# The causal mask of an attention block added by VectorE in PSUM, in place of a matmul of the identity with the mask

## The chip, the cores and the metric

The kernel runs on one core of a Trainium2 chip. The metric is the device time of one execution in microseconds (us), taken as the median of several runs. Engines: PE is TensorE's matmul stream and PEld its weight loads, DVE is VectorE, ACT is ScalarE, POOL is GpSimd, and SP is the queue from which every DMA of this kernel is issued. SBUF is the on-chip memory, PSUM the buffer that matmuls write.

## What is computed

Two layers of a decoder trunk with four token mixers in parallel. The part that matters here is branch B, causal attention with 8 heads over 1024 tokens, with 96 columns per query and key:

```
def one_block(args):
    q_blk, blk = args
    s = jnp.einsum('bhtd,bshd->bhts', q_blk, k).astype(jnp.float32) * scale
    query_pos = blk * ATTN_BLOCK + jnp.arange(ATTN_BLOCK)
    s = jnp.where(key_pos[None, :] <= query_pos[:, None], s, -jnp.inf)
    p = jax.nn.softmax(s, axis=-1).astype(v.dtype)
    return jnp.einsum('bhts,bshd->bthd', p, v)
```

Queries are taken in blocks of 128. Block t sees keys 0 to 128(t+1)-1, and only its last 128 columns, the diagonal block, need a mask.

## The kernel before

**Precision.** Operands are split into a high and a low part, and a product is three matmuls (high by high, high by low, low by high) accumulated in PSUM. Names ending in h and l are such parts: fh and fl are the two parts of the queries or keys of a head, bh and bl (wh and wl) those of a weight block.

**Attention.** `attention` runs over 8 heads and two halves b of the sequence, 16 steps to a layer. A step has a front and a back. The front, for the four query tiles t = 4b to 4b+3 of the next step, is `attn_scores` (three matmuls for each 512 columns into a tile named mm, then the mask, the row maximum mx on DVE at L1054, and ACT's nm, the maximum times the scale) and `attn_probs` (ACT's exponential into a tile pr, read straight from the PSUM tile mm). There are two mm buffers, so scores of tile t+2 wait until the exponential of tile t has been read out. The back, `attn_values`, transposes the four pr tiles on PE (L1087) into a PSUM tile tr, copies tr on ACT to the high part of pT, subtracts on DVE (L96) to get its low part, and multiplies both with the values v into the tile pv. There are two tr buffers. The 8 heads by 8 query tiles by 2 layers make 128 tiles.

**The mask.** A 128x128 bf16 tile `maskb` holds 0 on and below the diagonal and -1e30 above it. The last matmul of each score tile multiplies the bf16 identity with it and adds the result onto the diagonal block.

**Background.** While attention runs, the kernel also computes gate branches that later stages need (`background`). Each is two half blocks of 24 matmuls into a PSUM tile bg, a DVE product into bgx, ACT's tanh, and for the gate of branch B three more DVE operations. The last of these multiplies bgx with bgr, the inverse row sums of the softmax, which take a way through memory: a reciprocal and a copy (rows) on DVE, a DMA to riscr, and a DMA back that spreads them over the partitions (L164). br is the raw weight block of a background, with a single buffer, bh its cast on DVE and bl its low part, made by POOL.

**What sets the order.** The program is written in the order of the source. A scheduler with its own estimates of durations then sets the order of each engine's queue; background matmuls have a low priority and are put where it expects PE to wait. Each engine, and SP, works through its queue in that order, and an instruction that waits holds up everything behind it. A change of one instruction therefore moves others.

Of the kernel before, what the change touches and what calls it, by code (L numbers as in the profile page):

```python
# [15 lines left out]
MUL, ADD, SUB = ALU.mult, ALU.add, ALU.subtract  # L16

P = 128
# [26 lines left out]
class Trunk:  # L45
# [990 lines left out]
    def attn_scores(self, head, t, qt, kT):  # L1036

        nc = self.nc
        kh, kl = kT
        at = head % 2 * 8 + t  # L1040
        sc, nsc, sm = [x[:, at:at + 1] for x in (self.qs[head // 2], self.nqs[head // 2], self.asum[head // 2])]
        n = (t + 1) * P
        qh, ql = [x[0:96, t * P:(t + 1) * P] for x in qt]
        ps = self.mm()
        for c0 in range(0, n, 512):
            w = max(min(512, n - c0), 256)
            o = ps[:, c0:c0 + w]
            last = c0 + 512 >= n
            self.mmr(o, qh, kh[0:96, c0:c0 + w], True, False)
            self.mmr(o, qh, kl[0:96, c0:c0 + w], False, False)  # L1050
            self.mmr(o, ql, kh[0:96, c0:c0 + w], False, not last)
        self.mmr(ps[:, n - P:n], self.identb, self.maskb, False, True)
        mx, nm = self.ss(1, "mx"), self.ss(1, "nm")
        nc.vector.reduce_max(out=mx, in_=ps[:, 0:n], axis=AX.X)  # L1054
        self.act(nm, mx, AF.Identity, scale=nsc)
        return ps, n, nm, sc, sm
# [610 lines left out]
```

## Time and profile before

| | |
|---|---|
| median of 3 runs | 2439.56 us (2437.25 to 2441.05) |
| the profiled execution | 2440.25 us |
| its span, first to last instruction | 2438.5 us |
| mean granted TensorE clock | 0.988 |
| attention of layer 0 | about 516 to 755 us |
| attention of layer 1 | about 1700 to 1932 us |

The two stretches of attention are where the changed lines run. The busy time of PE counts a matmul until its modelled end, which reaches into the next one: two matmuls in a row start 0.23 us apart when they have 512 columns, though each is shown as 0.39 us long. What a matmul costs is therefore read from the distance between starts, and a wait that is shorter than the overlap doesn't show as idle time.

### The profile page before, as it was taken

The numbers are of one execution on the slowest core, as the hardware profiler recorded it, in microseconds if no ns is written. First come the engines' busy times: TensorE is split into PE (matmuls) and PEld (weight loads), VectorE is DVE, ScalarE is ACT, GpSimd is POOL, SyncE is SP. The second block draws the span as 40 slices with busy tenths as digits, with TensorE's granted clock in tenths as the row PEclk, the third lists the DMA queues.
The fourth block names the chain that finished last, engine by engine and source line by source line (L and its number), as shares of the span: only waits on it lengthen the run. The fifth ranks groups of instructions, "written<-read, shape, count | busy, mean of one in ns | idle before, by whom it ended". The sixth has DMA issues, their size and how long they took to land. (4 is left out here: it accounts for less than half of the span.)

```text
span 2438.5 us, 28178 instructions
## 1 busy us (share of the span) xinstructions
PE 2325.2 (95%) x11174; PEld 1855.2 (76%) x11174; DVE 1215.9 (50%) x1871; ACT 706.5 (29%) x1233; POOL 775.0 (32%) x605
## 2 busy tenths in 40 slices
PE   7998889989999999999999888999999999999999
PEld 5766677867778888888877666787777888888887
DVE  6455784366676323236244556714666652233351
ACT  4121253247762101101111213522577420111010
POOL 3533113432304214342435421143322132244411
PEclk9999999999999999999999999999999999999999
DMA  4226343242332112222432363413423211122342
GB/s 153 75 93 184 115 138 102 82 123 79 95 106 66 61 44 70 69 77 105 156 100 73 96 188 108 139 49 103 125 83 109 80 44 52 56 92 79 103 156 69
DMA packets 91700, 237.56 MB, mean 97 GB/s; under 512 B 25200, under 2 KB 34352, under 8 KB 91568
## 3 DMA queue, kind: packets, MB, share of 16 engines
q1 hardware_dynamic: 91568, 235.76, 30.4%
q8 instruction: 88, 1.44, 0.2%
q14 instruction: 44, 0.36, 0.1%
HBM read 175.27 MB, written 60.46 MB: 97 GB/s over the span
## 5 line engine op out<-in xcount | busy, mean ns | idle before, releaser
L96 POOL TENSOR_TENSOR wl<-wr,wh 128x1024 fp32r<-128x1024 f32 (+3 forms) x125 | 295.9, 2367 | 946.1 <-DVE wh L152 634.7
L176 PE MATMUL mm<-xh,wh 128*128 128x512 f32 x1216 | 378.7, 392 | 9.1 <-ACT xh L106 8.7
L152 DVE CAST wh<-wr 128x1024 fp32r<-128x1024 f32 (+2 forms) x110 | 78.4, 713 | 618.6 <-PE mm L176 539.8
L176 PE MATMUL mm<-xh,wl 128*128 128x512 f32 x1216 | 376.1, 390 | 0.8 <-POOL wl L96 0.8
L176 PE MATMUL mm<-xl,wh 128*128 128x512 f32 x1216 | 376.8, 390 | 0.0
L176 PEld LDWEIGHTS mm<-xh,wh 128*128 128x128 f32 x1216 | 227.3, 188 | 59.9 <-ACT xh L106 8.7
L176 PEld LDWEIGHTS mm<-xh,wl 128*128 128x128 f32 x1216 | 228.3, 188 | 49.7 <-POOL wl L96 1.6
L176 PEld LDWEIGHTS mm<-xl,wh 128*128 128x128 f32 x1216 | 228.4, 188 | 49.0 <-issue 0.8
L176 PE MATMUL bg<-xh,bh 128*128 128x512 f32 x576 | 229.2, 416 | 15.5 <-DVE bgx L96 15.5
L176 PE MATMUL bg<-xl,bh 128*128 128x512 f32 x576 | 226.3, 411 | 0.0
L176 PE MATMUL bg<-xh,bl 128*128 128x512 f32 x576 | 224.1, 409 | 1.0 <-POOL bl L96 1.0
L96 POOL TENSOR_TENSOR bl<-br,bh 128x1024 fp32r<-128x1024 f32 x36 | 96.4, 2678 | 317.0 <-DVE bh L152 203.3
L106 ACT ACTIVATE cmn<-cmn,bmh 128x1024 f32<-128x1024 f32 x44 | 50.6, 1151 | 440.7 <-DVE cmn L96 440.7
L96 DVE TENSOR_TENSOR pT<-tr,pT 128x512 fp32r<-128x512 f32 x224 | 125.6, 571 | 42.8 <-ACT pT L106 42.1
L176 PEld LDWEIGHTS bg<-xh,bh 128*128 128x128 f32 x576 | 111.8, 195 | 46.0 <-DVE bgx L96 25.6
L176 PE MATMUL pv<-pT,v 128*128 128x512 f32 (+3 forms) x384 | 134.0, 388 | 7.9 <-DVE pT L96 5.1
L106 ACT ACTIVATE pT<-tr 128x512 fp32r<-128x512 f32 x224 | 111.0, 505 | 86.6 <-PE tr L1087 77.3
L176 PEld LDWEIGHTS bg<-xh,bl 128*128 128x128 f32 x576 | 111.1, 193 | 24.9 <-issue 3.2
L1054 DVE TENSOR_REDUCE mx<-mm 128x1 f32<-128x128 f32 (+7 forms) x128 | 96.5, 754 | 64.5 <-PE mm L176 63.7
L176 PEld LDWEIGHTS bg<-xl,bh 128*128 128x128 f32 x576 | 111.3, 194 | 21.8 <-issue 4.0
L106 ACT ACTIVATE pr<-mm,nm,qs 128x128 f32<-128x128 f32 (+7 forms) x128 | 106.3, 830 | 0.9
L1087 PE MATMUL tr<-ident,pr 128*128 128x128 f32 x576 | 97.9, 275 | 0.3 <-ACT pr L106 0.2
(449 smaller groups left out, 4173.7 us busy)
## 6 DMA issues: line engine op xcount, KB each, us to landing
wr<-in_w_cm_dram SPq DMA_DIRECT2D x76, 512.0 KB, 3.6
br<-in_w_cm_dram SPq DMA_DIRECT2D x36, 512.0 KB, 3.7
bgscr<-bgx SPq DMA_DIRECT2D x20, 512.0 KB, 3.1
gate<-bgscr SPq DMA_DIRECT2D x20, 512.0 KB, 5.6
ysscr<-bgx SPq DMA_DIRECT2D x16, 512.0 KB, 2.6
br<-ysscr SPq DMA_DIRECT2D x16, 512.0 KB, 3.4
wr<-in_w_out_dram SPq DMA_DIRECT2D x16, 512.0 KB, 3.7
bgr<-riscr SPq DMA_DIRECT2D x24, 256.0 KB, 4.8
```

Source lines behind the costliest of these rows:

```text
L96: (eng or self.nc.vector).tensor_tensor(out=out, in0=x, in1=y, op=op)
L106: self.nc.scalar.activation(out, x, f, **k)
L152: self.nc.vector.tensor_copy(hi[:, :n], raw)
L176: self.nc.tensor.matmul(out, lhsT, rhs, start=start, stop=stop)
L1054: nc.vector.reduce_max(out=mx, in_=ps[:, 0:n], axis=AX.X)
L1087: nc.tensor.transpose(pt[:, k * P:(k + 1) * P], pts[k][:, st * P:(st + 1) * P], self.ident)
```

## The change

The mask matmul is gone, and the last score matmul closes the accumulation. DVE adds maskb (bf16, SBUF) onto the diagonal 128x128 of the PSUM tile, in place, and the row maximum follows as before. `tt` is the helper at L95 and L96 that issues a tensor_tensor on DVE, so the new operation is recorded at L96.

```
             w = max(min(512, n - c0), 256)
             o = ps[:, c0:c0 + w]
-            last = c0 + 512 >= n
             self.mmr(o, qh, kh[0:96, c0:c0 + w], True, False)
             self.mmr(o, qh, kl[0:96, c0:c0 + w], False, False)
-            self.mmr(o, ql, kh[0:96, c0:c0 + w], False, not last)
-        self.mmr(ps[:, n - P:n], self.identb, self.maskb, False, True)
+            self.mmr(o, ql, kh[0:96, c0:c0 + w], False, True)
+        self.tt(ps[:, n - P:n], ps[:, n - P:n], self.maskb, ADD)
```

The scheduler then orders the queues anew. Three places in layer 0 show it. Numbers in the names tell tiles apart and are the same in both programs; after the change, lines below the edit are one lower.

DVE, in the third head, where the scores of the tiles mm_4349 and mm_4371 are reduced. Before:

```order
L96 TENSOR_TENSOR pT_4335<-tr_4330,pT_4335 128x512
L96 TENSOR_TENSOR bgx_4535<-bg_4536,rsb_557 128x512
L96 TENSOR_TENSOR pT_4344<-tr_4340,pT_4344 128x384
L1054 TENSOR_REDUCE mx_4357<-mm_4349 128x1
L96 TENSOR_TENSOR pT_4366<-tr_4363,pT_4366 128x256
L1054 TENSOR_REDUCE mx_4379<-mm_4371 128x1
```

The same place after the change:

```order
L96 TENSOR_TENSOR pT_4335<-tr_4330,pT_4335 128x512
L1053 TENSOR_REDUCE mx_4325<-mm_4317 128x1
L96 TENSOR_TENSOR pT_4344<-tr_4340,pT_4344 128x384
L96 TENSOR_TENSOR mm_4349<-mm_4349,maskb_218 128x128
L1053 TENSOR_REDUCE mx_4357<-mm_4349 128x1
L96 TENSOR_TENSOR pT_4366<-tr_4363,pT_4366 128x256
L96 TENSOR_TENSOR pT_4385<-tr_4383,pT_4385 128x128
L96 TENSOR_TENSOR mm_4371<-mm_4371,maskb_218 128x128
```

In 90 of the 128 tiles the add stands directly ahead of its reduction; in the others something comes between, mostly one pT operation (as for mx_4325, which before stood ahead of pT_4335) or a product into bgx. The product into bgx_4535 has moved to another place.

PE, at the change from half 0 to half 1 of the same head's values, between the scores of mm_4399 and mm_4408, the first two tiles of the next step. Before:

```order
L1087 MATMUL tr_4426<-ident_204,pr_4390 128x128
L176 MATMUL bg_4562<-xl_23_135,bh_4531 128x512
L176 MATMUL bg_4562<-xh_22_134,bl_4532 128x512
L176 MATMUL bg_4562<-xh_25_144,bh_4531 128x512
L176 MATMUL bg_4562<-xl_26_145,bh_4531 128x512
L176 MATMUL bg_4562<-xh_25_144,bl_4532 128x512
L176 MATMUL mm_4408<-fh_4296,wh_4288 128x256
```

The same place after the change:

```order
L1086 MATMUL tr_4426<-ident_204,pr_4390 128x128
L176 MATMUL bg_4562<-xh_28_154,bh_4531 128x512
L176 MATMUL bg_4562<-xl_29_155,bh_4531 128x512
L176 MATMUL bg_4562<-xh_28_154,bl_4532 128x512
L176 MATMUL bg_4562<-xh_31_164,bh_4531 128x512
L176 MATMUL bg_4562<-xl_32_165,bh_4531 128x512
L176 MATMUL bg_4562<-xh_31_164,bl_4532 128x512
L176 MATMUL bg_4562<-xh_34_174,bh_4531 128x512
L176 MATMUL bg_4562<-xl_35_175,bh_4531 128x512
L176 MATMUL bg_4562<-xh_34_174,bl_4532 128x512
L176 MATMUL mm_4408<-fh_4296,wh_4288 128x256
```

Nine background matmuls stand ahead of mm_4408 where five stood; the others of the nine stood a little earlier, ahead of mm_4399.

SP, the DMA queue, after the row sums of a pair of heads are written to riscr. Before:

```order
L1074 DMA riscr<-rows_4526 16x128
L1019 DMA wr_4835<-q2scr 96x1024
L1239 DMA ybscr<-yb_4071 128x1024
L1019 DMA wr_4839<-kscr 96x1024
L1028 DMA wr_4845<-vscr 128x512
L1275 DMA bgy_4591<-ybscr 128x1024
L149 DMA br_6103<-in_w_cm_dram 128x1024
L164 DMA bgr_4594<-riscr 64x1024 x2
```

The same place after the change:

```order
L1073 DMA riscr<-rows_4526 16x128
L1019 DMA wr_4835<-q2scr 96x1024
L1238 DMA ybscr<-yb_4071 128x1024
L1019 DMA wr_4839<-kscr 96x1024
L1274 DMA bgy_4591<-ybscr 128x1024
L164 DMA bgr_4594<-riscr 64x1024 x2
L1028 DMA wr_4845<-vscr 128x512
```

The load of the row sums, bgr, has moved ahead of the load of a head's values (wr from vscr), and the load of a weight block (br) that stood ahead of it now comes before riscr.

## Rows read from the trace of the kernel before

**Rows 1.** The page's part 1: busy us (share of the span), instructions.

```profile
PE 2325.2 (95%) x11174; PEld 1855.2 (76%) x11174; DVE 1215.9 (50%) x1871; ACT 706.5 (29%) x1233; POOL 775.0 (32%) x605
```

**Rows 2.** Busy time by stretch: PE, PEld, DVE, ACT, POOL, then clock, DMA.

```profile
560.00:600.00 40.00, 39.17 (x220) 29.87 (x220) 27.03 (x44) 30.30 (x71) 13.47 (x7) 1.00 0.36 106
1690.00:1730.00 40.00, 34.00 (x149) 25.36 (x149) 26.84 (x52) 15.72 (x30) 13.08 (x6) 0.91 0.37 106
```

**Rows 3.** The tile view of maskb: count, durations (ns, min/median/max), first and last start.

```profile
L176 PE MATMUL mm<-maskb,identb x128: 229/232/330, 516.2 to 1907.9; 128*128 128x128 bf16 x128
```

**Rows 4.** Timeline of PE around two mask matmuls: start us, us, instruction.

```profile
562.41 0.23 PE L176 MATMUL mm<-maskb,identb 128*128 128x128 bf16 x1
562.48 0.39 PE L1087 MATMUL tr<-ident,pr 128*128 128x128 f32 x2
...
539.15 0.23 PE L176 MATMUL mm<-maskb,identb 128*128 128x128 bf16 x1
539.20 0.48 PE L176 MATMUL bg<-xh,bh 128*128 128x512 f32 x1
539.51 0.40 PE L176 MATMUL bg<-xl,bh 128*128 128x512 f32 x1
539.75 0.39 PE L176 MATMUL pv<-pT,v 128*128 128x512 f32 x1
```

**Rows 5.** Groups by shape on DVE, 580 to 680 us: busy us, mean ns.

```profile
L96 DVE TENSOR_TENSOR pT<-tr,pT 128x256 fp32r<-128x256 f32 x8 | 3.4, 419 | 0.3 <-ACT pT L106 0.3
L96 DVE TENSOR_TENSOR pT<-tr,pT 128x128 fp32r<-128x128 f32 x8 | 2.3, 285 | 2.0 <-ACT pT L106 2.0
```

**Rows 6.** Timeline: two dependent DVE operations, then one tile's chain.

```profile
527.02 0.23 DVE L103 SCALAR_TENSOR_TENSOR ry<-rt,ry 128x64 f32<-128x64 f32 x1
527.27 0.23 DVE L96 TENSOR_TENSOR ry<-ry,pre 128x64 f32<-128x64 f32 x1
...
562.68 1.09 DVE L1054 TENSOR_REDUCE mx<-mm 128x1 f32<-128x896 f32 x1 [0.53 <-PE mm L176]
```

**Rows 7.** Tile views of pr and pv: waits on them, us in total, times.

```profile
PEld mm L176: 18.3, 34
PE mm L176: 7.3, 6
...
DVE pT L96: 19.6, 45
```

**Rows 8.** Timeline: the bgr load of one gate, and who waits for it.

```profile
590.68 3.47 POOL L96 TENSOR_TENSOR bl<-br,bh 128x1024 fp32r<-128x1024 f32 x1
594.18 0.33 SPq L149 DMA_DIRECT2D br<-in_w_cm_dram  x1
594.62 1.09 SPq L164 DMA_DIRECT2D bgr<-riscr  x2
601.09 1.23 DVE L96 TENSOR_TENSOR bgx<-bgx,bgr 128x1024 f32<-128x1024 f32 x1 [2.98 <-DMA bgr<-riscr]
602.97 0.50 PE L176 MATMUL pv<-pT,v 128*128 128x512 f32 x1 [2.39 <-DVE pT L96]
```

**Rows 9.** Timeline: three more waits of PE that a gate of branch B causes.

```profile
651.21 0.50 PE L176 MATMUL pv<-pT,v 128*128 128x512 f32 x1 [1.52 <-DVE pT L96]
...
589.36 0.50 PE L176 MATMUL bg<-xh,bh 128*128 128x512 f32 x1 [0.54 <-DVE bgx L96]
...
638.43 0.50 PE L176 MATMUL bg<-xh,bh 128*128 128x512 f32 x1 [0.53 <-DVE bgx L96]
```

**Rows 10.** Timeline: waits of PE where each layer's attention begins.

```profile
528.79 0.44 PE L176 MATMUL mm<-fh,wh 96*128 96x384 f32 x1 [2.13 <-ACT pr L106]
...
537.58 0.50 PE L176 MATMUL mm<-fh,wh 96*128 96x512 f32 x1 [1.19 <-ACT pr L106]
...
1707.86 0.80 PE L176 MATMUL bg<-xh,bh 128*128 128x512 f32 x1 [2.99 <-DVE bgx L96]
...
1720.47 0.44 PE L176 MATMUL mm<-fh,wh 96*128 96x384 f32 x1 [2.65 <-ACT pr L106]
```

## Prediction, made before the changed kernel ran

> **What bounds the kernel now.** The page's busy times come first: PE is shown busy for 95% of the span, the next engine, DVE, for 50% [rows 1]. So an edit that takes work off PE and gives it to DVE looks like a plain gain. But the changed lines run only in the two attention stages, some 470 us together, so the stretches there are read next [rows 2]. In a settled stretch (560 to 600 us) PE is shown busy 39.17 of 40 us, ACT 30.30 and DVE 27.03; at the head of layer 1's attention (1690 to 1730) PE is down to 34.00 and the granted clock to 0.91. There PE's queue stops for chains that run through DVE and ACT. The third view is who waits. Over the program PE and its weight loads waited 34 + 6 times, 18.3 + 7.3 us, for ACT's exponential (pr) before they could overwrite a score tile, and 45 times, 19.6 us, for DVE's low parts of pT [rows 7]. The new operation lengthens exactly these two chains. So attention is bound by PE's queue with short stops in it, and the question is whether the stops grow by more than the queue shrinks.
>
> [...]
>
> **Term 1: the matmul removed.** There are 128 [rows 3]. Their shown 232 ns is not their price, since matmuls overlap. The starts tell it [rows 4]: from the mask matmul at 562.41 to the transpose at 562.48 is 0.07 us. Where a 512-column matmul follows, the mask at 539.15 is followed at 539.20, and that matmul takes 0.31 us to its successor, against 0.24 for the one after it (539.51 to 539.75): 0.05 + 0.07 = 0.12. In the timeline a transpose follows in 103 of the 128 cases. 103 x 0.07 + 25 x 0.12 = 7.2 + 3.0 = 10.2 us less in PE's queue. It can be worth nothing where PE stops anyway: -10.2 to 0, taken -10.2, since background matmuls fill most stops and what they fill here is saved after attention.
>
> **Term 2: the chain to the exponential.** DVE gains 128 adds of 128x128 with one operand in PSUM. The nearest row is pT's subtraction of that shape, 285 ns; it writes SBUF, and no row has DVE writing PSUM, so the upper end is the next shape, 419 ns [rows 5]. A dependent operation starts 0.25 after one of 0.23 [rows 6], so the reduction starts about 0.02 to 0.03 after the add ends. The mask matmul's start to the reduction's was 0.27 (562.41 to 562.68) [rows 4, 6], and the add can start after the last score matmul just as the reduction did after the mask, 0.07 sooner. Each tile's maximum is thus 0.285 + 0.03 - 0.07 = 0.24 us later (0.38 at the upper end). Where that lands: at the 40 waits for pr [rows 7], 40 x 0.24 = 9.6 us at most, 15.2 with the slow add, 0 if all are covered. Of the 40, one per head lies where half 0 gives way to half 1, 16 in all, and there the new order on PE puts nine background matmuls, about 2 us, ahead of the waiting scores, where five stood. That covers 0.24. The rest: 24 x 0.24 = 5.8, taken.
>
> **Term 3: DVE's queue.** An add that waits at the head of DVE's queue for PE's scores holds back the pT subtractions behind it, and PE's value product waits for those. The reduction waited in the same place before, so what is new is 0.31 us of work. At the 45 waits for pT [rows 7] it is 14 us at most and nothing at the least, as DVE has 13 of 40 us free [rows 2]. I take 2. Where a pT or a bgx operation now stands between add and reduction the maximum is later by another 0.3 to 1.2; the order shows 38 such tiles, and it is the same 40 waits that could feel it, inside the bounds of term 2.
>
> **Term 4: the heads of the stages.** In both layers the first adds stand inside DVE's chain of small operations that makes the scales, and PE waits for its end (2.13 and 2.65 us) [rows 10]: two adds of about 0.2 us beyond the gaps that they fill, 0.8 for both layers. In layer 1 a cast of a weight block now stands ahead of the two products into bgx for which PE waits 2.99: 0.7, and the add there 0.2. Together +1.7. Against that, in layer 0 the wait of 1.19 at 537.58 now has some dozen background matmuls ahead of it: -1.2. Ends: 0 and -1.2, +3 and 0.
>
> **Term 5: what the new order moves.** This is not in the edit's lines. The load of the row sums bgr for a gate was held on SP behind a weight block's load (br), which waited until POOL had freed its buffer (590.68 + 3.47 = 594.15, br at 594.18, bgr at 594.62). It landed at about 601, DVE stood for 2.98 us, and PE then for 2.39 [rows 8]. In the new order the cast and bl of that block come some 15 us earlier, br is loaded ahead of riscr, and bgr follows at once on the load of the keys, before the values. So it lands well before DVE asks. The second pair of heads has the same pattern (1.52), and the two short waits for bgx at 589.36 and 638.43 (0.54, 0.53) belong to the same queueing [rows 9]. Sum: -(2.39 + 1.52 + 0.54 + 0.53) = -5.0; at the least 0, if DVE's queue finds another place to stand. The load of the values that is now behind bgr has time: its data is wanted in the next head, over 15 us later, and if that cover went, POOL and ACT would pass the delay on to the next head's first product. In layer 1 these loads keep their order; I count nothing there.
>
> **The sum.** -10.2 + 5.8 + 2.0 + 1.7 - 1.2 - 5.0 = -6.9 us. The profiled execution took 2440.25 (span 2438.5), so 2433.4; it lies 0.7 above the median of the runs, 2439.56, so 2432.7. A walk by hand through one head (562.41 to 585.16) with these durations and the new order ends 0.14 us later than before, but with 28 background matmuls done instead of 23: 5 x 0.23 - 0.14 = 1.0 us gained, of which the eight masks are 0.6. That says terms 2 and 3 are rather too high than too low.
>
> **Rivals.** *PE's gain falls into waits.* If attention runs at the pace of the chain through DVE and ACT, term 1 is worth 0 and the rest stays: 5.8 + 2.0 + 1.7 - 1.2 - 5.0 = +3.3, 2442.9. For it: ACT is busy for 30 of 40 us and PE waits 45 times for pT. Against it: PE is shown idle for less than 1 of those 40 us. Chance 0.26.
>
> *DVE's queue becomes the bound.* DVE goes from 27 to about 30.5 of 40 us (some 11 tiles x 0.31). If nearly every one of the 40 + 45 waits grows by the add and the loads of term 5 save nothing, the sum is 9.6 + 14 + 1.7 - 10.2 = +15.1, 2454.7. It decides once the waits grow by more than 15 of the possible 24 us. For it: 38 reductions stand behind something else. Against it: the walk through a head. Chance 0.17.
>
> *The chains are covered altogether.* Terms 2 and 3 at 0: -10.2 + 1.7 - 1.2 - 5.0 = -14.7, 2424.9. For it: the walk. Against it: the waits of 0.2 to 0.5 us before each second score tile were there with background matmuls ahead of them too. Chance 0.14. That the change doesn't do what it says is ruled out: the orders hold 128 adds and no mask matmul.
>
> **How the numbers follow.** The forecast, 2432.7, has 0.43. Some 0.2%, 4.9 us, is what a measurement of this kernel can tell from no change: faster is below 2434.7, slower above 2444.4. Nearly all of the forecast's chance (0.38) and all of the covered case is faster: 0.52. The first rival and the rest of the forecast are same: 0.31. Slower is 0.17. The range leaves out the slow rival and takes in the others, from 2424 to 2444.
>
> **What would show it.** Right: PE without the 128 mask matmuls, 128 operations mm<-mm,maskb on DVE near 285 ns, a reduction 0.31 after each add; the waits of 2.39 and 1.52 gone, bgr landing long before its product; waits for pr up by some 6 us in total; fewer background matmuls left after attention. Wrong: an add of 400 ns or more; the waits of PE for pT or pr up by over 15 us; new waits of PE of over 1 us behind bgx in either layer; or a lower granted clock over a longer stretch at the heads of the stages, where it is 0.91 now [rows 2].

## The result, and the profile after

The changed kernel takes 2452.41 us (median of 6 runs, 2448.97 to 2453.66), beside 2438.18 for the kernel before (6 runs, 2435.14 to 2441.05). The ratio is 1.0059, with a 95% interval of 1.0049 to 1.0069: 14.4 us slower, where 6.9 faster was forecast. It lies above the range of 2424 to 2444. The profiled execution took 2453.66 us (span 2451.9), 13.4 more than the one of before. In what follows a difference in microseconds is the ratio of a run's time to that of the kernel before on the same chip, less 1, times 2438. Its interval is 2 to 3 us to either side, and about 4 for the difference of two such numbers.

The busy times of the whole program (page, part 1, as [rows 1]) say nothing of this. PE is shown as busy as before, DVE has 128 operations and 37 us more.

```profile
PE 2326.6 (95%) x11046; PEld 1869.5 (76%) x11046; DVE 1252.6 (51%) x1999; ACT 711.7 (29%) x1233; POOL 771.3 (31%) x605
```

The stretch that was settled before ([rows 2]; PE, PEld, DVE, ACT, POOL, clock) now has PE 2.0 us less busy, DVE 4.2 busier, and the granted clock at 0.96 instead of 1.00:

```profile
560.00:600.00 40.00, 37.17 (x192) 29.84 (x191) 31.18 (x56) 28.67 (x66) 11.47 (x6) 0.96 0.40 119
```

The tile view of maskb (count, durations in ns, first and last start; as [rows 3]) has the adds. One takes 298 ns, close to the 285 that the prediction took:

```profile
L96 DVE TENSOR_TENSOR mm<-mm,maskb x128: 277/298/300, 516.7 to 1921.8; 128x128 f32<-128x128 f32 x128
```

The tile views of pr and pv (waits on them, us in total, times; as [rows 7]) show which chain got longer. The sums take waits of PE and waits of its weight loads together, and one stop can be counted in both. The waits for the exponential are 24.9 us where they were 25.6. Those for the low parts of pT went from 19.6 us in 45 waits to 32.1 in 53. Those for its high parts, which ACT copies and which the prediction did not look at, nearly doubled too. Before:

```profile
ACT pT L106: 13.5, 34
```

After:

```profile
PEld mm L176: 19.4, 53
PE mm L176: 5.5, 12
...
DVE pT L96: 32.1, 53
ACT pT L106: 25.9, 39
```

The list of DVE's waits for DMAs (us in total, times, the longest) shows what became of the gates' loads. The waits for bgr, 15.3 us in 6 before, are down to 5.0, and those for bgy, the branch's result read back from memory, have gone up from 2.2 us in 2:

```profile
DVE bgx L103 <- DMA bgy<-ybscr: 10.1, 6, 5.8
...
DVE bgx L96 <- DMA bgr<-riscr: 5.0, 4, 2.0
```

In the gate of [rows 8], DVE now stands 1.61 us for bgy instead of 2.98 for bgr, and PE 1.45 instead of 2.39 (timeline: start, us, instruction, idle time before it; in all timelines here, lines between those shown are left out):

```profile
592.77 1.23 DVE L103 SCALAR_TENSOR_TENSOR bgx<-bgx,bgy 128x1024 f32<-128x1024 f32 x1 [1.61 <-DMA bgy<-ybscr]
595.32 0.50 PE L176 MATMUL pv<-pT,v 128*128 128x512 f32 x1 [1.45 <-DVE pT L96]
```

Behind that stop the granted clock falls to 0.51, where the kernel before has 1.00 in the same stretch (columns as above):

```profile
596.00:599.50 3.50, 3.50 (x14) 3.13 (x13) 2.44 (x4) 1.10 (x3) 0.00 (x0) 0.51 0.30 126
```

In the next pair's gate PE stops 1.26 us, at 644.88, where it stopped 1.52 [rows 9].

The longest of DVE's waits makes PE's longest wait in attention; the timelines show how. In the new order the product bgx<-bgx,bgy of the third pair's gate stands directly behind the pT operation of 686.42. Its data was asked for at 683.04, behind two weight blocks, and DVE stood for 5.81 us. The adds and maxima of the next tiles stood behind it, ACT waited 5.51 for the maximum with the copies of pT behind that in its own queue, and so PE stood for 5.97:

```profile
681.40 1.59 SPq L149 DMA_DIRECT2D wr<-in_w_av_dram  x2
683.04 0.42 SPq L1274 DMA_DIRECT2D bgy<-ybscr  x1
...
686.42 0.28 DVE L96 TENSOR_TENSOR pT<-tr,pT 128x128 fp32r<-128x128 f32 x1
692.50 1.23 DVE L103 SCALAR_TENSOR_TENSOR bgx<-bgx,bgy 128x1024 f32<-128x1024 f32 x1 [5.81 <-DMA bgy<-ybscr]
...
694.30 0.29 ACT L106 ACTIVATE nm<-mx,nqs 128x1 f32<-128x1 f32 x1 [5.51 <-DVE mx L1053]
695.27 1.52 PE L176 MATMUL pv<-pT,v 128*128 128x512 f32 x2 [5.97 <-ACT pT L106]
```

The other place is the end of attention and the head of the stage behind it. (Layer 0's attention ends, by its last value product, at about 719 us in the kernel before and 726 in the changed one, and layer 1's at about 1920 and 1934; the 755 and 1932 given for the kernel before are too late.) PE stops five times between 719 and 730. Behind the stop of 0.97 us its 256-column matmuls still run 0.12 us apart (728.04 to 728.16), and behind the next, of 1.25, they run 0.21 apart (26 steps from 730.18 to 735.73):

```profile
719.55 0.51 PE L176 MATMUL pv<-pT,v 128*128 128x512 f32 x1 [0.77 <-DVE pT L96]
...
724.54 0.50 PE L176 MATMUL pv<-pT,v 128*128 128x512 f32 x1 [0.45 <-DVE pT L96]
727.82 0.39 PE L176 MATMUL mm<-wkh,xh 128*128 128x256 f32 x1 [0.97 <-DVE wkh L152]
728.04 0.28 PE L176 MATMUL mm<-wkh,xl 128*128 128x256 f32 x1
728.16 0.28 PE L176 MATMUL mm<-wkh,xh 128*128 128x256 f32 x1
729.80 0.58 PE L176 MATMUL mm<-wkl,xh 128*128 128x256 f32 x1 [1.25 <-DVE wkl L96]
730.18 0.41 PE L176 MATMUL mm<-wkh,xh 128*128 128x256 f32 x1
730.40 0.41 PE L176 MATMUL mm<-wkh,xl 128*128 128x256 f32 x1
```

Busy time over that stretch (the clock is 0.69; it is 0.50 from 730.2 to 735.9 by itself, and 1.00 from 728 to 729):

```profile
726.00:737.00 11.00, 8.71 (x46) 8.18 (x46) 6.13 (x10) 0.63 (x2) 2.37 (x1) 0.69 0.62 202
```

Layer 1 has the same five stops (0.77, 0.22, 0.46, 0.97 and 1.24 us), and there the granted clock is 0.84 (1936 to 1947 us).

In the kernel before, 8 background matmuls were left over when layer 0's attention ended and 18 in layer 1. The 8, and 11 of the 18, filled these waits (in layer 0, 0.55 and 0.45 us remained at wkl); the other 7 stood later, in the merges, where the gates' results are joined. Now none is left in either layer.

**A table by step.** ACT's 16 copies of pv into yt in each layer mark the ends of attention's 16 steps. For each step I take its length, less 0.23 us for each background matmul that PE did in it (that work is only moved), and compare with the kernel before. "Head" is the time from the last step's end to the 90th matmul of the next stage. The columns after the second are experiments told of below.

| us against before | after | e1 | e2 | e3 | e5 | e6 | e7 | e14 |
|---|---|---|---|---|---|---|---|---|
| layer 0, steps 0 to 12 | -1.9 | +0.1 | -3.5 | -4.9 | -3.6 | -4.7 | +0.1 | -8.6 |
| step 13 | +7.1 | +0.2 | +5.6 | -0.1 | +2.5 | +3.9 | +0.2 | -0.6 |
| step 14 | -0.5 | +0.4 | -0.5 | -0.4 | -0.5 | -0.5 | +0.4 | -0.2 |
| step 15 and head | +7.0 | 0.0 | +7.0 | 0.0 | +5.7 | +5.6 | +5.1 | +0.5 |
| layer 1, steps 0 to 11 | -3.9 | +1.9 | +2.4 | -3.0 | -4.2 | -5.4 | +1.7 | -2.4 |
| step 12 | +3.2 | +0.7 | +3.5 | -0.1 | +3.1 | -0.3 | +0.8 | +0.5 |
| steps 13 and 14 | -0.1 | +0.5 | -0.3 | -0.6 | -0.1 | +3.2 | +0.5 | +2.0 |
| step 15 and head | +6.6 | 0.0 | +6.7 | 0.0 | +6.7 | +6.7 | +4.3 | 0.0 |
| sum | +17.4 | +3.8 | +20.8 | -9.2 | +9.7 | +8.5 | +13.0 | -8.8 |

These are single executions, and the first step alone differs by 1 to 2 us between executions of the same order. The sums follow the measured times within some 6 us. For the changed kernel the table reads at once: over the first 13 and 12 steps it gains 5.8 us, and it loses 23.8 in four places: step 13 of layer 0, step 12 of layer 1, and the end in both. That the gain is near the forecast is luck: in e1, which has the edit in the old order, these steps are 2.0 us longer, so the gain came with the order and not with the edit.

Part of the loss is the clock behind the stops. The mean granted clock is 0.95 from 510 to 740 us where the kernel before has 0.99, and 0.97 from 1690 to 1950 where it has 0.99; e1 has 0.99 in both. How much of the time this makes, beside the stops themselves, is not parted here.

### The profile page after: what moved, and what is told of

It is laid out like the page before. It is cut to its first block, busy times and chain, and to the rows that moved or that the text cites. A ratio compares the mean times of both kernels' runs of the same rounds, so it can differ in the third digit from the quotient of the medians.

```text
span 2451.9 us, 27971 instructions
## 1 busy us (share of the span) xinstructions
PE 2326.6 (95%) x11046; PEld 1869.5 (76%) x11046; DVE 1252.6 (51%) x1999; ACT 711.7 (29%) x1233; POOL 771.3 (31%) x605
## 5 line engine op out<-in xcount | busy, mean ns | idle before, releaser
L96 POOL TENSOR_TENSOR wl<-wr,wh 128x1024 fp32r<-128x1024 f32 (+3 forms) x125 | 296.8, 2374 | 953.8 <-DVE wh L152 654.2
L176 PE MATMUL bg<-xh,bh 128*128 128x512 f32 x576 | 228.6, 416 | 14.0 <-DVE bgx L96 13.9
L96 POOL TENSOR_TENSOR bl<-br,bh 128x1024 fp32r<-128x1024 f32 x36 | 94.1, 2614 | 322.9 <-DVE bh L152 216.9
L96 DVE TENSOR_TENSOR pT<-tr,pT 128x512 fp32r<-128x512 f32 x224 | 124.4, 570 | 30.7 <-ACT pT L106 29.7
L176 PEld LDWEIGHTS bg<-xh,bl 128*128 128x128 f32 x576 | 111.4, 194 | 23.8 <-issue 3.2
L176 PEld LDWEIGHTS pv<-pT,v 128*128 128x128 f32 x384 | 67.7, 192 | 54.9 <-DVE pT L96 21.2
```

The source lines that it names most:

```text
L96: (eng or self.nc.vector).tensor_tensor(out=out, in0=x, in1=y, op=op)
L176: self.nc.tensor.matmul(out, lhsT, rhs, start=start, stop=stop)
```

## The experiments

**Holding the order.** The change does two things at once: it replaces an operation, and it makes the scheduler set all queues anew. To part them, most kernels below hold each engine's queue in a given order. The two programs are traced in the same sequence, with an add where a mask matmul stood, so one order can be carried over to the other:

```
+def hold_order(tc):
+    ins = list(tc.nc.cur_bb.bb.instructions)
+    info = mybir.DependencyInfo(mybir.DependencyClass.NoSync, mybir.DependencyReason.DATA)
+    for e, v in _order().items():
+        for x, y in zip(v, v[1:]):
+            tc.add_manual_dep(ins[y], ins[x].name, info, reason="order")
```

In e1's trace DVE, ACT and POOL run the operations of the kernel before in the same sequence, with the 128 adds put in and nothing else moved. The kernel before, held in its own order, was not run; nearest to it is e8, which moves a few loads only, at +2.0 us (-0.5 to +4.1). "Old order" is that of the kernel before, "new order" that of the changed kernel.

| run | mask | order | ratio to before (95%) | us |
|---|---|---|---|---|
| changed kernel | add | new | 1.0059 (1.0049 to 1.0069) | +14.4 |
| e1 | add | old | 1.0024 (1.0014 to 1.0033) | +5.9 |
| e2 | matmul | new | 1.0064 (1.0051 to 1.0076) | +15.6 |
| e3 | none | old | 0.9967 (0.9953 to 0.9980) | -8.0 |
| e4 | both | old | 1.0039 (1.0026 to 1.0052) | +9.5 |
| e13 | none, side add | old | 0.9997 (0.9986 to 1.0007) | -0.7 |
| e5 | add | new, 1 product later | 1.0043 (1.0031 to 1.0055) | +10.5 |
| e6 | add | new, 4 products later | 1.0036 (1.0023 to 1.0049) | +8.8 |
| e7 | add | old, background early | 1.0078 (1.0065 to 1.0091) | +19.0 |
| e8 | matmul | old, bgr early | 1.0008 (0.9998 to 1.0017) | +2.0 |
| e9 | add | new, end old | 1.0088 (1.0074 to 1.0101) | +21.5 |
| e10 | add | e6 and e9 | 1.0068 (1.0056 to 1.0081) | +16.6 |
| e11 | add | own, 11 branches | 1.0009 (0.9999 to 1.0020) | +2.2 |
| e12 | matmul | own, 11 branches | 1.0028 (1.0017 to 1.0040) | +6.8 |
| e14 | add | own, 12 branches | 0.9987 (0.9977 to 0.9996) | -3.2 |
| e15 | matmul | own, 12 branches | 1.0018 (1.0008 to 1.0028) | +4.4 |
| e16 | add | own, 14 branches | 1.0059 (1.0046 to 1.0072) | +14.4 |

### The edit or the order: e1 to e4

e1 is the changed kernel with `hold_order(tc)` behind `t.run()` and the old order, each add directly ahead of its maximum:

> The edit alone: the matmul of the mask is out and the add is in, as in the changed kernel, but every engine's queue is held in the order of the kernel before; each add stands directly ahead of its row maximum. Theory 'order' (the loss came from the queues' new order, and the add itself is nearly paid for by the matmul that is gone): 2430 to 2439 us. Theory 'add' (0.3 us more in DVE's queue for each tile lengthens the waits in whatever order): 2447 to 2455 us. The prediction's terms 1 to 4 without term 5 and without the two reordered heads come to about 2436.

e2 is the kernel before with the new order, each mask matmul directly behind its tile's last score matmul:

> The order alone: the mask is added by the matmul, as in the kernel before, and DVE has no adds, but every engine's queue is held in the order of the changed kernel (each mask matmul directly behind the last score matmul of its tile). Theory 'order': as slow as the changed kernel or slower, 2450 to 2462 us. Theory 'add': back to about the kernel before, 2433 to 2442 us, the waits behind the adds being gone.

e3 and e4, both in the old order:

```
e3:
-        self.tt(ps[:, n - P:n], ps[:, n - P:n], self.maskb, ADD)
e4:
         self.mmr(ps[:, n - P:n], self.identb, self.maskb, False, True)
+        self.tt(ps[:, n - P:n], ps[:, n - P:n], self.maskb, ADD)
```

> Left out: the causal mask altogether (no matmul and no add), in the order of the kernel before. It prices the 128 mask matmuls by themselves. By the distances between starts they are worth 10.2 us where PE is the bound everywhere: 2428 us. If PE's gain falls into waits: 2436 to 2439 us. Both theories on the loss have room for either; the difference to the run with the add in the same order is the price of the adds: 2 to 8 us by 'order', 14 us or more by 'add'.

> Both: the mask matmul stays and DVE adds the mask once more (the values stay the same to softmax), in the order of the kernel before. It prices the 128 adds on top of the kernel before. 'Order': +2 to +8 us, 2440 to 2446 us. 'Add': +18 us or more, 2456 us and above.

Measured: +5.9, +15.6, -8.0 and +9.5. e1 came out at 2445.01 us and e4 at 2447.98, between the numbers of the two theories, so neither theory is the whole. The edit alone costs 5.9 us. The order alone, without a single add, costs 15.6; on top of the edit it makes 14.4 - 5.9 = 8.5. The matmuls are worth 8.0 where no add takes their place, and 9.5 - 5.9 = 3.6 where the adds are there; with some 4 us of uncertainty on the second number, that they are worth less there is likely but not shown. The adds cost 5.9 + 8.0 = 13.9 where the prediction had 5.8 + 2.0.

### Which of the adds' two terms: e13

e13 keeps the adds' load on DVE's queue and takes it off the chain to the exponential:

```
-        self.tt(ps[:, n - P:n], ps[:, n - P:n], self.maskb, ADD)
         mx, nm = self.ss(1, "mx"), self.ss(1, "nm")
         nc.vector.reduce_max(out=mx, in_=ps[:, 0:n], axis=AX.X)
+        self.tt(self.side, ps[:, n - P:n], self.maskb, ADD)
```

> Left out: the causal mask (as in e3, no matmul and no add into the scores), in the order of the kernel before. In its place DVE makes, directly behind each row maximum, an add of the same shape from the same PSUM tile into a scrap tile that nothing reads. It takes the same 0.3 us of DVE's queue as e1's add, but the maximum doesn't wait for it. Theory 'queue' (the adds' price of 13.8 us, e1 less e3, is paid by what stands behind them in DVE's queue, the low parts of pT; the prediction's term 3): as slow as e1 or nearly, 2440 to 2446 us. Theory 'chain' (it is paid by the exponential that comes later; term 2): as fast as e3, 2429 to 2434 us.

It came out at -0.7 us, halfway from e3 to e1, so both terms count: the queue's load costs -0.7 + 8.0 = 7.3 us and the later maximum 5.9 + 0.7 = 6.6, each with some 4 us of uncertainty. The side add took 281 ns. The waits tell where the two land (waiting engine and tile, what it waited for, us in total, times, the longest). e3, then e13, then e1:

```profile
ACT nm L106 <- DVE mx L1052: 11.6, 20, 1.4
...
PEld pv L176 <- DVE pT L96: 13.7, 43, 2.4
PE pv L176 <- DVE pT L96: 3.4, 3, 2.0
```

```profile
ACT nm L106 <- DVE mx L1053: 13.7, 22, 1.4
...
PEld pv L176 <- DVE pT L96: 20.4, 61, 1.8
PE pv L176 <- DVE pT L96: 3.6, 9, 1.4
```

```profile
ACT nm L106 <- DVE mx L1053: 23.8, 38, 1.7
...
PEld pv L176 <- DVE pT L96: 28.0, 73, 1.9
PE pv L176 <- DVE pT L96: 5.6, 12, 1.5
```

The waits for pT's low parts go from 17.1 us (13.7 + 3.4) to 24.0 and 33.6. Most of them are waits of weight loads; PE's own go from 3.4 to 3.6 and 5.6. The first step is DVE's queue. With the second, ACT's operation nm waits 10 us more for the later maxima. The copies that begin the next pT stand behind nm in ACT's queue, but that the delay reaches PE by them is argued, not shown: DVE's own waits for these copies fell, from 31.3 us in e13 to 27.7 in e1. The waits for pr, where the prediction looked for the later maximum, did not grow with it (17.5 + 5.0 us in e3, 20.4 + 8.6 in e13, 15.8 + 5.2 in e1).

### Where DVE stands: e5 and e6

The new order is kept; in e5 one operation of DVE goes back, shown by its place in the queue:

```
 pT_5787 <- tr_5785
-bgx_5625 <- bgx_5625, bgy_5681
 mm_5801 += maskb, mx_5806, yb_5706, mm_5810 += maskb
 pT_5825, mx_5815, pT_5833
+bgx_5625 <- bgx_5625, bgy_5681
```

> The changed kernel with its order held, except for one DVE operation: the product bgx<-bgx,bgy of the third pair's gate in layer 0, behind which DVE stood for 5.81 us for the load of bgy and PE for 5.97, goes three places of DVE's queue later, where the kernel before has it (behind the next two subtractions of pT). Theory 'a place to stand' (the loss of this step is that one product's place): the step of the third pair gets 5 to 7 us shorter, 2446 to 2448 us. Theory 'stands elsewhere' (DVE or PE stops for the same data a little later): 2450 to 2453 us.

Step 13 is 4.5 us shorter, and the run 3.9 (+10.5 for +14.4), which is about the uncertainty of such a difference; 2448.88 us lies just beyond the first theory's numbers. The data still comes late, but DVE stands for 1.12 and PE for 2.03:

```profile
694.20 1.23 DVE L103 SCALAR_TENSOR_TENSOR bgx<-bgx,bgy 128x1024 f32<-128x1024 f32 x1 [1.12 <-DMA bgy<-ybscr]
...
696.86 0.50 PE L176 MATMUL pv<-pT,v 128*128 128x512 f32 x1 [2.03 <-DVE pT L96]
```

The clock belongs to this price. From 690 to 706 us the changed kernel had 0.79, in and behind the stop of 5.97 (0.67 up to 695 us, 0.84 from there), and e5 had 1.00 (first row after, second row e5):

```profile
690.00:706.00 16.00, 10.73 (x49) 8.42 (x50) 10.65 (x20) 6.95 (x19) 0.00 (x0) 0.79 0.18 56
```

```profile
690.00:706.00 16.00, 13.31 (x75) 10.73 (x75) 11.79 (x22) 8.85 (x23) 0.00 (x0) 1.00 0.25 72
```

e6 deals with another kind of stop. In the changed kernel the product bgx<-bgs,bgx, which takes 1.22 us, took 3.83 in step 12 of layer 1, and 2.65 and 2.80 at two places in layer 0. Each time POOL was at work. (Such a thing is not new: in the kernel before one of these products, at 1737.37, took 2.68 beside POOL.) The timeline of the worst:

```profile
1888.95 2.40 POOL L96 TENSOR_TENSOR fl<-wr,fh 96x1024 fp32r<-96x1024 f32 x1 [12.98 <-ACT fh L106]
1889.85 3.83 DVE L103 SCALAR_TENSOR_TENSOR bgx<-bgs,bgx 128x1024 f32<-128x1024 f32 x1
1891.31 1.30 POOL L96 TENSOR_TENSOR v<-wr,v 128x512 fp32r<-128x512 f32 x1
1893.61 0.94 DVE L1053 TENSOR_REDUCE mx<-mm 128x1 f32<-128x768 f32 x1
```

POOL's two operations end at 1892.61 and the product at 1893.68, 1.07 later. The other two, at 572.56 and 622.14, end 1.07 and 1.08 after POOL's bl. e6 moves these three products behind the next two pT operations, besides e5's:

```
 mx_14669
-bgx_14579 <- bgs_14632, bgx_14579
 mx_14681, pT_14691, pT_14700
+bgx_14579 <- bgs_14632, bgx_14579
```

> As e5, and three more products of DVE (bgx<-bgs,bgx of the first and second pair in layer 0 and of the third pair in layer 1) go behind the next two subtractions of pT. In the changed kernel they took 2.65, 2.80 and 3.83 us where such a product takes 1.22, and each ended about 1.1 us after POOL's operation that was running. Theory 'DVE is held while POOL runs': they take 1.2 to 1.3 us again, PE's waits of 0.83, 0.77 and 2.07 us behind them go, 2 to 4 us less than e5: 2443 to 2446 us. Theory 'it is slow for another reason' (its data): the products stay long and e6 is as long as e5.

The products took their 1.22 us again, at 573.32, 622.50 and 1882.76, where POOL was idle:

```profile
1882.76 1.22 DVE L103 SCALAR_TENSOR_TENSOR bgx<-bgs,bgx 128x1024 f32<-128x1024 f32 x1
```

That these three products were held while POOL ran is shown: 2.65, 2.80 and 3.83 us beside it, 1.22 away from it. The reverse is seen in the gate of [rows 8]: there bl and the product begin together (590.68), the product takes 1.23 and bl 3.47, where bl takes 2.39 to 2.40 beside the products that it holds. The time, 1.7 us less than e5, is less than the interval: steps 3 and 7 of layer 0 got 1.1 us shorter each, but in layer 1 the 3.4 us saved in step 12 came back in step 13 (+3.3), where DVE now stood 2.04 for bgy. The product of 3.83 also stood through POOL's second operation, which began when the first ended. That is not always so: in e11 a product bgx<-bgx,bgr at 633.87 ran between fl and v, the same two operations of POOL (1.86 us), and the second of them then took 2.25 (1.30 in the timeline above).

### Cover that is used up: e7, e9 and e10

In e7 the old order and the add stay, and only PE's background matmuls move (numbers are places in PE's queue):

```
 layer 0, last half block of bg:
-2992 to 3004, then 3017, 3018, 3030, 3031, 3038, 3040, 3045 to 3049, 3054 to 3056
+2992 to 3004 and directly behind it the other 14
 layer 1: 20 in the same way
```

> The run e1 (the edit in the order of the kernel before), with one change of PE's order: the last 14 (layer 0) and 20 (layer 1) background matmuls of the last gate, which stood as fillers in the last step of attention and behind it, are brought forward into one block near the head of that step, so that, as in the changed kernel, none is left for its end. Theory 'cover used up': the last step and the head of the next stage get longer by 2 to 6 us in each layer, 2449 to 2457 us. Theory 'it does not matter where the background stands': 2443 to 2447 us, as e1.

It cost 13.1 us (+19.0 for +5.9), more than any other change of place that was tried. The waits at the head of layer 0's next stage are those of the changed kernel to the hundredth, and the clock falls too (0.88 from 712 to 740 us; e1 has 1.00 from 707 to 735):

```profile
724.54 0.38 PE L176 MATMUL mm<-wkh,xh 128*128 128x256 f32 x1 [0.97 <-DVE wkh L152]
726.53 0.58 PE L176 MATMUL mm<-wkl,xh 128*128 128x256 f32 x1 [1.25 <-DVE wkl L96]
```

```profile
712.00:740.00 28.00, 25.25 (x149) 21.96 (x148) 16.69 (x21) 6.58 (x11) 4.79 (x2) 0.88 0.38 128
```

Of the 13.1 the table shows 9.4 in the last steps and heads. Seven of the 20 in layer 1 had stood as fillers in the merges; that the rest is theirs is argued, not shown.

e9 and e10 try the repair: the new order (in e10 with e6's four moves) up to the last value product of step 14, all queues in the old order behind that.

> The changed kernel, with its own order up to the end of the last step but one of attention in each layer; from there to the end of the layer every queue is in the order of the kernel before. The 11 background matmuls that are left there then stand between the value products of the last step and behind it instead of in one block ahead of them. It is the repair that answers to e7. Theory 'cover used up': most of what e7 lost (11 us) comes back, though 11 matmuls cover less than the 21 and 29 of the kernel before: 2442 to 2447 us. Theory 'the rest of the order': 2450 to 2454 us.

> e9 and e6 together: the four DVE products later, and the end of attention in the order of the kernel before. If the two causes add, e6's 5.9 us and e9's gain go together: 2436 to 2441 us, no slower than the kernel before. If they share the same waits: 2443 to 2447 us.

Both expectations failed. By their ratios e9 and e10 are 7 and 8 us slower than their counterparts without the repair (3.6 and 8 by the profiled executions). Only 11 background matmuls of the last half block are left at that point in either layer, where the old order had 24. Taken together, steps 14 and 15 and the head of layer 0 need 1.2 us less in e9 than in the changed kernel, with the same 16 matmuls in them; in layer 1 they need as long as in the changed kernel, with 9 matmuls in place of 16, so 7 more are left to be done later. So the loss doesn't come from the place of the last 11, and few matmuls cover little wherever they stand; that fits a stock that is used up but doesn't show it. Why both got slower than without the repair isn't settled.

### More cover: e11, e12 and e14 to e16

```
-BG = [(1, c) for c in range(8)] + [(3, c) for c in range(6, 8)]
+BG = [(1, c) for c in range(8)] + [(3, c) for c in range(5, 8)]
```

is the edit of e11 and e12; range(4, 8) is that of e14 and e15, range(2, 8) that of e16. Each branch moves 48 matmuls of a layer from the merges to the background, with the scheduler's own order.

> The changed kernel with one gate branch more computed as background (branch M, column block 5, so 11 instead of 10; 48 matmuls per layer move from the merges into attention). The scheduler sets its order anew. Theory 'cover used up': with 48 matmuls more there is some left for the end of attention, and the changed kernel gains more by it than the kernel before does (e12): 2440 to 2447 us. Theory 'DVE's queue': the branch brings DVE more operations and nothing is gained, 2450 to 2458 us.

> The kernel before with the same gate branch more as background: the control for e11. By 'cover used up' it gains little, as it has 8 and 18 matmuls left over at the end of attention already: 2436 to 2442 us. If background matmuls fill waits all over attention it gets as much faster as e11: 2428 to 2434 us.

> The changed kernel with two gate branches more as background (branch M, column blocks 4 and 5: 12 instead of 10), the scheduler's own order. With 11 some 29 and 32 background matmuls were left over at the end of attention, so by 'cover used up' there is nothing more to gain from cover: 2438 to 2443 us, as e11. If more background keeps filling waits: 2430 to 2436 us, which would be a version faster than both.

> The kernel before (mask matmul) with 12 background branches: the control for e14. If the gain of e14 comes from the cover that the adds need, the kernel before gains nothing by it, as with 11: 2438 to 2445 us. If 12 branches help any kernel: 2430 to 2436 us.

> The changed kernel with 14 background branches (branch M, column blocks 2 to 7). With 12 some 80 and 100 background matmuls were left over at the end of attention, so attention has no use for more: by 'cover used up' as e14 within 0.2%, 2431 to 2439 us. If later stages use the background as cover too: 2426 to 2431 us.

With 11 branches the changed kernel is 12.2 us faster than with 10, with 12 it is 17.6 faster, and at 2434.76 us (2431.33 to 2438.47, 11 runs) it is faster than both kernels, than the one before by 3.2 us (1.0 to 5.6). The kernel before gets slower by the same edits (+6.8, +4.4), so the gain isn't that of background as such. In e14's column the four places that cost the changed kernel 23.8 us cost 0.4, with 82 and 104 matmuls left over when attention ends; at wkl PE waits 0.59 us where it waited 1.25:

```profile
719.58 0.38 PE L176 MATMUL mm<-wkl,xh 128*128 128x256 f32 x1 [0.59 <-DVE wkl L96]
```

At the two ends of attention, where e7 shows the same from the other side, cover is thus what the changed kernel lacked. At steps 13 and 12 it may be cover or the places of single products in the new order, as in e5 and e6; that isn't parted here. Nor is what e14 did better than expected, or what the kernel before lost by the same edit; both may again be the luck of a new order. With 14 branches the changed kernel is back at +14.4. Its attentions are no longer than e14's; the stretches behind them, up to the next attention and to the end, are 13.6 and 12.7 us longer. There the background matmuls follow each other closely, and PE waits for DVE to read out bg: 30.7 us in 34 waits in the whole program where e14 has 19.6 in 23, nearly all of the difference behind the attentions:

```profile
PE bg L176 <- DVE bgx L96: 30.7, 34, 4.1
```

What makes the rest of that loss is open.

### Term 5 by itself: e8

e8 is the kernel before in its own order, except on SP, where bgy and bgr of layer 0's gates go ahead of the load of values or weights; a fourth buffer lets them.

```
-        self.fp = mk(name="fp", bufs=3)
+        self.fp = mk(name="fp", bufs=4)
-NU = 38
+NU = 37
```

> The kernel before in its own order, with the mask matmul, and term 5 of the prediction by itself: a fourth buffer for the gates' tiles (and one less of the 38 large ones), and on SP the loads of bgy and bgr of the three gates in layer 0 go ahead of the load of values or of a weight block. By term 5 the waits of PE behind bgr (2.39 and 1.52) and two short ones go: 2434 to 2437 us. If DVE finds another place to stand, or the saved time is lost to cover that background matmuls gave anyway: 2438 to 2442 us.

It gave +2.0 us, not the -5.0 of term 5. DVE no longer stood for bgr in the three gates. In the first that was worth what the prediction said: step 5 of layer 0, with the wait of 2.39 [rows 8], got 2.6 us shorter. In the second it was worth little (0.3 us less in step 9): the product bgx<-bgs,bgx begins within 0.01 us of POOL's bl and is held, and PE stops 1.39 for what stands behind it, where it stopped 1.52 [rows 9]. The two short waits that term 5 counted stayed, at 0.53 each.

```profile
638.81 3.47 DVE L103 SCALAR_TENSOR_TENSOR bgx<-bgs,bgx 128x1024 f32<-128x1024 f32 x1
638.82 2.39 POOL L96 TENSOR_TENSOR bl<-br,bh 128x1024 fp32r<-128x1024 f32 x1
643.03 0.47 PE L176 MATMUL pv<-pT,v 128*128 128x512 f32 x1 [1.39 <-DVE yb L96]
```

e1 shows the same exchange without touching a load. There too the waits of 2.39 and 1.52 are absent. An add now stands ahead of the product, POOL's bl begins first, the product takes 2.90 us (2.92 in the second gate, 1.23 in both before), and PE stands at the same gate for other things (0.80 at 588.22, 1.41 at 593.50):

```profile
588.22 0.51 PE L176 MATMUL bg<-xh,bh 128*128 128x512 f32 x1 [0.80 <-DVE bgx L96]
589.28 2.39 POOL L96 TENSOR_TENSOR bl<-br,bh 128x1024 fp32r<-128x1024 f32 x1
589.85 2.90 DVE L103 SCALAR_TENSOR_TENSOR bgx<-bgs,bgx 128x1024 f32<-128x1024 f32 x1
593.50 0.47 PE L176 MATMUL pv<-pT,v 128*128 128x512 f32 x1 [1.41 <-DVE yb L96]
```

Why e8 as a whole isn't faster is open. In its profiled execution the steps of attention are some 4 us shorter in sum, and attention begins 3.2 us later (515.85 for 512.64). The buffer that e8 takes from the large tiles may have its own price; that was not tried apart.

## Why the prediction was wrong, point by point

**What bounds the kernel** was read rightly: PE's queue with short stops. What was missing is that the stops are short because background matmuls fill them, and that these are a stock, of which 8 and 18 were left at the end. The prediction even used it ("background matmuls fill most stops") without asking when it runs out. It even named "fewer background matmuls left after attention" among the signs of being right. That sign came true, and the largest loss went with it.

**Term 1** (-10.2) holds: -8.0 in e3. With the adds in place, probably less of it comes through (3.6, with some 4 us of uncertainty).

**Term 2** (+5.8) has the right size (6.6) but the wrong place. With the later maximum the waits for pr did not grow; those for pT did. By which way the delay gets there, through ACT's queue or otherwise, is not shown.

**Term 3** (+2.0 of at most 14) was mis-sized: 7.3. The prediction leaned on DVE being free for 13 of 40 us. But 79 of the 192 pT operations of e1's attentions stand directly behind an add and its maximum, at the moment when DVE has work, and there a free third of the time is no help. With term 1's 2.2 and term 2's 0.8 this makes the edit +5.9 instead of -2.4.

**Terms 4 and 5** (+0.5 and -5.0) were the step that failed: they costed the new order at the places where it removes a wait, and it made 8.5 us more. The waits for bgr shrank, as said, and the waits of 2.39 and 1.52 went. But DVE then stood for bgy in the same gates, PE stopped 1.45 and 1.26 there, and with the lower clock behind the first stop these steps (5 and 9 of layer 0, measured as in the table) came out 0.8 and 0.1 us longer instead of 2.4 and 1.5 shorter. "If DVE's queue finds another place to stand" was written down as the case in which term 5 is worth 0. It was the case that came, and it cost time: one product now stands 5.81 us for bgy (e5: 3.9 us), three run into POOL's operations (e6: little by itself), and background matmuls that moved to the heads of steps, nine where five stood, are missing at the end (e7; 13.5 us in the table, against 7.8 gained in the steps ahead, after against e1). In layer 1 PE's wait of 2.99 for bgx [rows 10] became 3.55, about as forecast; the waits of 2.13 and 2.65, which the adds were to lengthen, are now 2.12 and 0.38. The walk through one head was right for its head; the loss lay in steps that it did not cover.

**The rivals.** "DVE's queue becomes the bound" came near the time (2454.7; its sum leaves out term 4's -1.2, with which it is 2453.5) by half of its mechanism, which is luck: the waits for pT's low parts did grow, by 12.5 us, those for pr did not, so together they stayed below the 15 at which it was to decide, and the other half is the order. "PE's gain falls into waits" is what e4 and e1 suggest in part. Of the signs that were named as wrong, the waits for pT or pr came true once ACT's copies are counted (12.5 + 12.4 - 0.7 us); the lower clock came true, but at 596, 690 and 726 us, while the head of layer 1's attention kept its 0.91; and new waits of over 1 us came, for pT and weights rather than bgx.

## What to carry to other kernels

An operation given to a less busy engine costs what it delays behind it in that engine's queue, and once more what waits for its result (here 7.3 and 6.6 us); the engine's free share over a stretch bounded neither. Where a scheduler sets the order, an edit and the order that it brings are two changes: hold the order and measure them apart before judging the edit, and count the filler work that is left at the end of the stage. Here the edit needed two more background branches to be worth making (2434.76 us).

## What the runs showed of the hardware that was not expected

- Three products bgx<-bgs,bgx of DVE, 1.22 us long at the median, took 2.65, 2.80 and 3.83 us beside POOL's operations bl, bl and fl, the last through POOL's next operation too, each ending 1.07 or 1.08 us after POOL. Behind the next two pT operations, all three took 1.22. Where the product and POOL's bl began within 0.01 us of each other, one of the two was longer: bl in the kernel before (3.47 for 2.39 to 2.40 us, at 590.68 and 639.78), the product in e8 (3.47 for 1.22). The timelines show the 3.83 and both 3.47 as longer operations with no idle time ahead of them, and lists of waits don't have them.
- With a single stop of PE of 5.97 us, and with a series of short ones at the end of attention, the changed kernel had a stretch at a lower granted clock (0.79 from 690 to 706 us, 0.69 from 726 to 737). The longer stop did not always have the lower clock: behind 1.45 us at 595.32 the clock was 0.51 (596 to 599.5), and in e5, with a stop of 2.03, it was 1.00 (690 to 706). Behind 729.80 some 6 us of matmuls ran 0.21 us apart instead of 0.12 (728.04 to 728.16), which is 2.7 us: more than either wait ahead of it.
- An add of 128x128 in place in PSUM, with a bf16 operand from SBUF, took 298 ns (median of 128, changed kernel); into SBUF it took 281 (e13).
